# An RWKV time-mixing kernel on one Trainium2 core: small copies and memsets from VectorE to GpSimd, loads one unit sooner, one store placed after a transpose instead of ahead of it

## The chip, the cores and the metric

The kernel runs on one core of a Trainium2 chip. The metric is the device time of one execution in microseconds (us). Work is spread over TensorE (PE in the profile, with its weight loads as PEld), VectorE (DVE), ScalarE (ACT), GpSimd (POOL) and SyncE (SP); transfers are issued by SP, ACT and POOL and carried by the core's 16 DMA engines.

## The reference

```python
batch, seq_len, d_model = (16, 2048, 256)
x_prev[:, 1:, :] = x[:, :-1, :]          # x_prev[:, 0, :] = 0
xv = x * time_mix_v + x_prev * (1 - time_mix_v)
xr = x * time_mix_r + x_prev * (1 - time_mix_r)
v = xv.reshape(-1, d_model) @ value_weight
r = xr.reshape(-1, d_model) @ receptance_weight
out = (1 / (1 + np.exp(-r)) * v) @ output_weight
```

The key branch of the model does not reach the output. Input and output are fp32, 32 MB each way in all.

## The kernel before, in words

The 16 batches are cut into 64 units of 512 tokens, four units to a batch. A unit needs x transposed, with the 256 channels on partitions in two halves (`ko`), because the three projections contract over channels. It also needs each token's predecessor. The transposed tile `xt` therefore keeps a row of slots of 128 tokens, and one additional slot, slot 0 of the row, that holds the last slot shifted by one token. Its first column is the zero that stands before a sequence (a memset, L224 for batches 0 and 1, L221 later); its other 127 columns are copied from the last slot by `wrap_slots` (L528), the "shifted slot" of the title.

Three stages make `xt`. Batches 0 and 1 are loaded unit by unit (L171, L189, L149), batches 2 to 9 whole (L159), and TensorE transposes them into PSUM (L297 and L269), from where ScalarE copies them (L302, L279, L286). Batches 10 to 15 are loaded as bf16 into DRAM (`x_natural`, L155 and L159) and transposed by two DMA transposes (L251), one for batches 10 to 12, issued in the pass g = 27, one for 13 to 15, in g = 39.

In the pass g of the main loop TensorE computes the receptance product of unit g (L364, `psum_r`), ScalarE its sigmoid (L629), TensorE the value product (L364, `psum_v`) and the output product of the unit before (L393, `psum_o`), ScalarE copies the output (L442) and SP stores it, two units at a time (L445, L411). The mixing is folded: x times a coefficient plus x_prev. VectorE makes one half of the scaling (L334), GpSimd the other (L344), and VectorE adds (L356) and multiplies sigmoid and value (L668). For unit 0 the receptance product is made from x and x_prev directly (`project_unmixed`, L378), which reads slots 0 to 3 of `xt[0]`.

Every engine executes in the order in which the code lists its instructions: the order is written out by hand (`tc.manual_schedule()`), and semaphores make an instruction wait for what it reads. So it matters where a statement stands. `new_xt(0)`, which holds the memset of slot 0 of batch 0, is called after the early loads:

```python
    for e in (2, 3):
        op = nc.gpsimd.dma_start(out=x_first[:, e - 2], ...)     # L189
        if e == 2:
            tc.add_manual_dep(op.ins, first_weight.ins.name, SYNC, ...)
    nc.gpsimd.dma_start(out=wo_bf, ...)                           # L192
    load(1)                                                       # L149, four transfers
    ...
    warm_up(WARM)                                                 # TensorE
    ...
    new_xt(0)                                                     # L224
```

The dependency on `first_weight` makes the first of these GpSimd transfers wait until the receptance weight has landed. `first_transposes`, with the transposes of unit 0, and then L549 (the weight of x_prev), L334, L356 and L378 follow.

In the late part, `STAGE_AT` says in which pass g the loads of batches 13 to 15 are issued; each waits for the first DMA transpose. `FIRST` lists the stores (by the unit that completes them) that are issued on SP ahead of a transpose, and that wait for half of the last load; `WAITING` lists those that are held until the transpose has been issued.

Of the kernel before, what the change touches and what calls it, by code (L numbers as in the profile page):

```python
# [15 lines left out]
def kernel(  # L16
# [25 lines left out]
    nc = tc.nc  # L42
# [10 lines left out]
    BYUNIT = 2  # L53
# [5 lines left out]
    FREE = CROSS  # L59
    LATE_O = CROSS - 2  # L60
    T_AT = {27: 10, 39: 13}
    FIRST = {21: 27, 27: 39, 29: 39}
    WAITING = {23: 27, 25: 27, 31: 39, 33: 39, 35: 39}
    ZEROS_AT = 12
    STAGE_AT = {33: 13, 34: 14, 35: 15}
    GROUPS = [(2, 3), (4, 5, 6), (7, 8, 9), (10, 11, 12), (13, 14, 15)]
    HALVED = (12, 15)
    PAD = 16
# [3 lines left out]
    AHEAD = 6  # L72
# [38 lines left out]
    xt = {}  # L111
# [2 lines left out]


    zeros = consts.tile([P, P], BF16)
    nc.vector.memset(zeros, 0.0)
    ident_f = consts.tile([P, P], FP32)
    make_identity(nc, ident_f)
    ident = consts.tile([P, P], BF16)  # L120
    nc.vector.tensor_copy(out=ident, in_=ident_f)

    def rows(b):
        return x[b].rearrange("(p j) d -> p j d", p=P)
# [39 lines left out]
    for m, tm in enumerate([time_mix_r, time_mix_v]):  # L164
        nc.scalar.dma_start(
            out=tm_rows[m * KO : (m + 1) * KO, :], in_=tm.rearrange("(ko p) -> ko p", p=P)
        )

    def load_halves(e):
# [8 lines left out]
        out=w_f32[:, 0], in_=receptance_weight.rearrange("(ko p) n -> p ko n", p=P)  # L178
# [28 lines left out]
    def new_xt(b):  # L207
        if b >= BYUNIT:
            for group in GROUPS:
                if b != group[0]:  # L210
                    continue
                if b >= STAGED:
                    t = xtpool.tile([P, KO, len(group) * (PAD + S)], BF16, name="xt_both")
                    for k in range(len(group)):
                        xt[b + k] = t[:, :, k * (PAD + S) + PAD - 1 : (k + 1) * (PAD + S)]
                    xt_both[b] = t
                    return
                xt_both[b] = xtpool.tile([P, J + 1, KO, len(group), P], BF16, name="xt_both")
                for k in range(len(group)):
                    xt[b + k] = xt_both[b][:, :, :, k]  # L220
                    nc.gpsimd.memset(xt[b + k][:, 0, :, 0:1], 0.0)  # L221
            return
        xt[b] = consts.tile([P, UB * (UJ + 1), KO, P], BF16, name=f"xt_first{b}")
        (nc.vector if b == 0 else nc.gpsimd).memset(xt[b][:, 0, :, 0:1], 0.0)  # L224

    new_xt(0)
    tms = consts.tile([P, 2, KO], FP32)
# [83 lines left out]
    def slots(piece, off=0):  # L311

        b, _, lo, hi = piece
        j = lo // P + (lo // TU if b < BYUNIT else 0) + off
        return slice(j, j + (hi - lo) // P)
# [56 lines left out]
    def project_unmixed(ps, mo):  # L372


        parts = [(w_prev[:, ko], ko, 0) for ko in range(KO)]
        parts += [(w_bf[:, 0, ko], ko, 1) for ko in range(KO)]
        for n, (w, ko, lo) in enumerate(parts):
            nc.tensor.matmul(  # L378
                out=ps[:, mo, :],
                lhsT=w[:, mo * P : (mo + 1) * P],  # L380
                rhs=xt[0][:, lo : lo + UJ, ko],
                start=(n == 0),
                stop=(n == len(parts) - 1),
            )
# [45 lines left out]
    def output(g, z):  # L430
# [19 lines left out]
        elif e % 2 == 1:  # L450
            pair = (b, (e - 1) * UJ, (e + 1) * UJ)
            if g in FIRST:
                firsts.setdefault(FIRST[g], []).append(pair)
            elif g in WAITING:
                kept.setdefault(WAITING[g], []).append(pair)
            else:
# [47 lines left out]
    def pieces(g):  # L504

        b, e = divmod(g, UB)
        tile_for(g // 2)
        return [(b, m, e * TU, (e + 1) * TU) for m in range(2)]

    def wrap_slots(piece, one=None, after=None):  # L510


        b, _, lo, _ = piece
        by_unit = b < BYUNIT
        key = (b, lo // TU if by_unit else UB - 1)
        if key not in late_copies:
            return
        kos = slice(0, KO) if one is None else slice(one, one + 1)
        if one in (None, KO - 1):
            late_copies.remove(key)  # L520
        j = slots(piece).start if by_unit else 0
        n = UJ if by_unit else J
        if by_unit and j > 0:
            engine = nc.vector if key == (0, 1) else nc.gpsimd
            engine.tensor_copy(out=xt[b][:, j, kos, 0:1], in_=xt[b][:, j - 1, kos, P - 1 : P])
        if key in shifted:
            return
        op = (nc.vector if after is None else nc.gpsimd).tensor_copy(  # L528
            out=xt[b][:, j, kos, 1:P], in_=xt[b][:, j + n, kos, 0 : P - 1]
        )  # L530
        if after is not None:
            tc.add_manual_dep(op.ins, after.ins.name, SYNC, reason="one at a time")
# [4 lines left out]
    def advance(limit):  # L537
        nonlocal tnext
        while tnext <= min(limit, NU - 1):
            b, e = divmod(tnext, UB)  # L540
            for n in LOADS.get((b, e), ()):
                loads[n] = load(n)
            if tnext < NU - BYDMA:
                transposes(tnext)
            tnext += 1

    first_transposes()
    for ko in range(KO):
        nc.vector.tensor_scalar(  # L549
            out=w_prev[:, ko, :],  # L550
# [6 lines left out]
        out=w_bf[:, 0, 0, :], in0=w_f32[:, 0, 0, :], scalar1=tms[:, 0, 0:1], scalar2=None, op0=ALU.mult  # L557
    )
    nc.scalar.activation(
        out=w_bf[:, 0, 1, :], in_=w_f32[:, 0, 1, :], func=ACT.Copy, scale=tms[:, 0, 1:2]  # L560
# [3 lines left out]
    for ko in range(KO):  # L564
        nc.vector.tensor_scalar(
            out=w_bf[:, 1, ko, :],
# [13 lines left out]
    pooled = {g: [] for g in range(-1, NU)}  # L580
# [36 lines left out]
    for g in range(NU - 1):  # L617
        ps_r = ps_r_pool.tile([P, KO, TU], FP32, name="psum_r")
        if g == 0:
            project_unmixed(ps_r, 0)  # L620
            advance(1)
            project_unmixed(ps_r, 1)
            wrap_slots(pieces(1)[0])
            scale(pieces(1)[0])
            last = add(pieces(1)[0])
        else:
            project(ps_r, g, 0)
        s_sb = zpool.tile([P, KO, TU], BF16, name="s_sb")
        nc.scalar.activation(out=s_sb, in_=ps_r, func=ACT.Sigmoid)  # L629
        advance(START_T[g] if g < len(START_T) else g + LOOK)  # L630
        if g in T_AT:
            half, whole = loads[T_AT[g] + 2]
            for pair in firsts.pop(g):
                store(nc.sync, *pair, after=half)
            last_t = by_dma(T_AT[g], whole)
            for pair in kept.pop(g, []):
                store(nc.sync, *pair)
        if LATE_O < g < NU - 2:
            output(g - 2, z_prev2)
        for p in products.get(g + 1, []):  # L640
            if g >= FREE and p[0][1] == 1:
                scale_act(p[0], (0,))
        for p in [q for q, _ in products[g]] + pooled[g]:
            last_unit_of = p[3] // TU - 1
            need = last_unit_of if p[0] < BYUNIT else min(last_unit_of + 1, UB - 1)
            assert UB * p[0] + need < tnext, (g, p, tnext)
            if g > AHEAD or p not in pooled[g]:
                wrap_slots(p)
        if g == 1:
            load(2)  # L650
            scale_act(pieces(2)[1], (1,))
        for p, kos in products[g]:
            if not (g - 1 >= FREE and p[1] == 1):
                scale(p, kos)
        for p in sums[g]:
            last = add(p)
        for p in pooled[g]:
            if p[0] >= BYUNIT:
                wrap_slots(p)
        ps_v = ps_v_pool.tile([P, KO, TU], FP32, name="psum_v")  # L660
        project(ps_v, g, 1)
        if g == 0:
            scale_act(pieces(1)[1], (0,))
            advance(2)
        z_sb = zpool.tile([P, KO, TU], BF16, name="z_sb")
        n = TU // 2 if g == NU - 2 else TU
        for c in range(0, TU, n):
            nc.vector.tensor_tensor(  # L668
                out=z_sb[:, :, c : c + n],
                in0=s_sb[:, :, c : c + n],  # L670
                in1=ps_v[:, :, c : c + n],
                op=ALU.mult,
            )
        for p in pooled[g]:
            wrap_slots(p, after=last)
            scale_pool(p, last)
        if ZEROS_AT <= g < ZEROS_AT + len(pads):
            zero_rows(*pads[g - ZEROS_AT])
        if g in STAGE_AT:
            b = STAGE_AT[g]  # L680
            loads[b] = load(b)
            for op in loads[b] if b in HALVED else [loads[b]]:
                tc.add_manual_dep(op.ins, last_t.ins.name, SYNC, reason="not beside transposes")
        for p in held[g]:
            add(p)
        if z_prev is not None and not LATE_O <= g < NU - 3:
            output(g - 1, z_prev)
        if g == 1:
            advance(4)
        z_prev2, z_prev = z_prev, z_sb  # L690
# [31 lines left out]
```

## Time and profile before

| what | value |
|---|---|
| median of 3 runs | 200.48 us (200.44 to 200.55) |
| the profiled execution | 201.01 us, of which the span from the first to the last instruction is 199.2 us |
| PE, DVE, ACT, POOL busy | 192.5, 184.4, 177.0, 86.9 us |
| granted TensorE clock, mean | 0.995 |
| DMA | 58.13 MB, mean 292 GB/s |

The span is 1.8 us shorter than the time of the same execution; that part lies around the program and is taken as fixed. Busy times are unions over an engine's instructions, so a busy share near 100% says that the engine had always something under way, not that it ran at its peak.

### The profile page before, as it was taken

What the parts mean: (1) busy time and instruction counts of PE and PEld (TensorE: products, weight loads), DVE (VectorE), ACT (ScalarE), POOL (GpSimd) and SP (SyncE); (2) the same over time, 40 slices, a digit from 0 to 9 for tenths busy, and PEclk for the clock granted to TensorE, in tenths of its full rate; (3) what the DMA queues carried; (4) which work ended last, traced back from release to release, by engine and by line L of the source; (5) the groups of instructions that cost most, each with busy time, mean ns of one, the idle gap of its engine ahead of it and who ended that gap; (6) DMA issues with size and microseconds to landing.
All of it is one profiled execution on the core that took longest, in us unless ns stands there. A gap on an engine that the chain in (4) does not pass through costs nothing.

```text
span 199.2 us, 3758 instructions
## 1 busy us (share of the span) xinstructions
PE 192.5 (97%) x1368; PEld 123.5 (62%) x1368; DVE 184.4 (93%) x289; ACT 177.0 (89%) x197; POOL 86.9 (44%) x115
## 2 busy tenths in 40 slices
PE   8999999999999999999999999999999999999990
PEld 3555676666666666666666556666666666666660
DVE  0899999999999999999999999999999999999960
ACT  3699899999999999999999999999999999999970
POOL 1656452453675635524424366444444444444200
PEclk9999999999999999999999999999999999999998
DMA  5799999999999999999999999999999999999994
GB/s 177 203 187 215 215 280 275 278 282 274 286 312 332 285 285 331 296 268 211 296 250 290 367 276 207 209 280 295 198 238 346 416 421 400 409 399 407 409 392 177
DMA packets 37961, 58.13 MB, mean 292 GB/s; under 512 B 26068, under 2 KB 27448, under 8 KB 35128
## 3 DMA queue, kind: packets, MB, share of 16 engines
q1 hardware_dynamic: 33392, 41.34, 60.7%
q0 software_dynamic: 4400, 16.44, 41.6%
q8 instruction: 10, 0.16, 0.3%
q10 hardware_dynamic: 152, 0.13, 0.2%
q14 instruction: 7, 0.06, 0.1%
HBM read 34.34 MB, written 39.90 MB: 373 GB/s over the span
## 4 chain that ended last, share of the span: by engine, by line
PE 88%; ACT 4%; DMA 2%; issue 2%; DVE 1%; SPq 0%; DVEq 0%
PE psum_v L364 26%; PE psum_o L393 26%; PE psum_r L364 26%; PE ps_t L269 8%; DMA w_f<-n_receptance_weight_dram 2%; ACT xt_first L286 1%; ACT s_sb L629 1%; PE psum_r L378 1%; PE ps_t L393 1%; ACT mix L609 1%; ACT o_sb L442 1%; PE ps_t L364 0%; SPq L171 0%; DVE z_sb L668 0%; DVE mix L356 0%
## 5 line engine op out<-in xcount | busy, mean ns | idle before, releaser
L344 POOL TENSOR_SCALAR mix<-xt_both,c_sb 128x1024 bf16<-128x1024 bf16 (+1 forms) x55 | 61.3, 1114 | 84.7 <-DVE mix L356 82.8
L356 DVE TENSOR_TENSOR mix<-mix,xt_both 128x1024 bf16<-128x1024 bf16 x112 | 77.4, 701 | 1.4
L668 DVE TENSOR_TENSOR z_sb<-s_sb,psum_v 128x1024 bf16<-128x1024 bf16 (+1 forms) x64 | 76.7, 1200 | 1.9 <-PE psum_v L364 0.8
L364 PEld LDWEIGHTS <-w_bf 128*128 128x128 bf16 x516 | 49.0, 98 | 38.7 <-DVE mix L356 0.5
L629 ACT ACTIVATE s_sb<-psum_r 128x1024 bf16<-128x1024 f32 x63 | 65.2, 1035 | 6.2 <-PE psum_r L364 6.0
L364 PE MATMUL psum_v<-mix,w_bf 128*128 128x512 bf16 (+1 forms) x256 | 65.3, 377 | 0.1
L364 PE MATMUL psum_r<-mix,w_bf 128*128 128x512 bf16 (+1 forms) x252 | 64.2, 377 | 0.0
L393 PE MATMUL psum_o<-wo_bf,z_sb 128*128 128x256 bf16 x486 | 63.4, 273 | 0.2 <-DVE z_sb L668 0.2
L393 PEld LDWEIGHTS <-z_sb 128*128 128x128 bf16 x512 | 51.7, 103 | 18.2 <-DVE z_sb L481 0.7
L442 ACT COPY o_sb<-psum_o 128x1024 f32<-128x1024 f32 x50 | 51.2, 1024 | 5.0 <-PE psum_o L393 5.0
L286 ACT COPY xt_both<-ps_t 128x1024 bf16<-128x1024 bf16 x32 | 32.8, 1036 | 0.0
L269 PEld LDWEIGHTS <-x_bf 128*128 128x128 bf16 x304 | 19.7, 98 | 8.9 <-DMA x_bf<-in_x_dram 1.5
L269 PE MATMUL ps_t<-ident,x_bf 128*128 128x128 bf16 x304 | 22.7, 219 | 0.3 <-DMA x_bf<-in_x_dram 0.3
L334 DVE TENSOR_SCALAR mix<-xt_both,c_sb 128x1024 bf16<-128x1024 bf16 (+1 forms) x47 | 21.1, 458 | 0.0
L609 ACT ACTIVATE mix<-xt_both,c_sb 128x1024 bf16<-128x1024 bf16 x14 | 16.3, 1161 | 0.0
L356 DVE TENSOR_TENSOR mix<-mix,xt_first 128x1024 bf16<-128x1024 bf16 x15 | 10.6, 713 | 0.1
L442 ACT COPY x_bf<-psum_o 128x1024 f32<-128x1024 f32 x10 | 10.2, 1015 | 0.0
L334 DVE TENSOR_SCALAR mix<-xt_first,c_sb 128x512 bf16<-128x512 bf16 x22 | 6.5, 348 | 0.3 <-ACT xt_first L279 0.2
L286 ACT COPY xt_first<-ps_t 128x1024 bf16<-128x1024 bf16 x6 | 6.2, 1027 | 0.0
L159 POOL DMA_DIRECT2D x_bf<-in_x_dram x8 | 5.7, 712 | 0.0
L528 POOL COPY xt_first<-xt_first 128x254 bf16<-128x254 bf16 x5 | 2.0, 395 | 6.6 <-DVE mix L356 6.6
L344 POOL TENSOR_SCALAR mix<-xt_first,c_sb 128x512 bf16<-128x512 bf16 x6 | 4.1, 689 | 0.7 <-DVE mix L356 0.2
(70 smaller groups left out, 54.0 us busy)
## 6 DMA issues: line engine op xcount, KB each, us to landing
out_dram<-o_sb SPq DMA_DIRECT2D x24, 1024.0 KB, 14.1
x_bf<-in_x_dram POOLq DMA_DIRECT2D x8, 1024.0 KB, 20.6
x_natural<-in_x_dram POOLq DMA_DIRECT2D x4, 1024.0 KB, 13.3
out_dram<-x_bf SPq DMA_DIRECT2D x4, 1024.0 KB, 13.1
x_natural<-in_x_dram POOLq DMA_DIRECT2D x4, 512.0 KB, 15.2
x_bf<-in_x_dram POOLq DMA_DIRECT2D x6, 256.0 KB, 6.1
out_dram<-x_bf SPq DMA_DIRECT2D x6, 256.0 KB, 4.2
o_sb<-in_x_dram SPq DMA_DIRECT2D x4, 256.0 KB, 4.0
```

Of the source, the lines that this page charges most:

```text
L159: return nc.gpsimd.dma_start(out=x_bf[b], in_=rows(b), max_dma_last_dim=run)
L269: nc.tensor.transpose(out=ps[:, jj], in_=src[:, jj, ko * P : (ko + 1) * P], identity=idn)
L286: nc.scalar.copy(out=xt[b][:, j0 : j0 + UJ], in_=ps)
L334: nc.vector.tensor_scalar(out=mixed(piece)[:, :, ko], in0=tokens(piece, 0, ko), scalar1=c_sb[:, m, ko : ko + 1], scalar2=None, op0=ALU.mult,)
L344: op = nc.gpsimd.tensor_scalar(out=mixed(piece)[:, :, 1], in0=tokens(piece, 0, 1), scalar1=c_sb[:, m, 1:2], scalar2=1.0, op0=ALU.mult, op1 ...
L356: return nc.vector.tensor_tensor(out=mixed(piece), in0=mixed(piece), in1=tokens(piece, 1), op=ALU.add)
L364: nc.tensor.matmul(out=ps[:, mo, :], lhsT=w_bf[:, m, ko, mo * P : (mo + 1) * P], rhs=mixed((b, m, e * TU + lo, e * TU + hi))[:, :, ko], st ...
L393: nc.tensor.matmul(out=ps[:, j, :], lhsT=slot[:, ko, j], rhs=wo_bf[:, ko, :], start=(ko == 0), stop=(ko == KO - 1),)
L442: nc.scalar.copy(out=o[:, j0 : j0 + UJ, :], in_=ps)
L609: nc.scalar.activation(out=mixed(piece)[:, :, ko], in_=tokens(piece, 0, ko), func=ACT.Copy, scale=c_sb[:, m, ko : ko + 1],)
L629: nc.scalar.activation(out=s_sb, in_=ps_r, func=ACT.Sigmoid)
L668: nc.vector.tensor_tensor(out=z_sb[:, :, c : c + n], in0=s_sb[:, :, c : c + n], in1=ps_v[:, :, c : c + n], op=ALU.mult,)
```

## The change

Five edits. The zero tile's memset (L117), the cast of the identity to bf16 (L121) and the memset of slot 0 of batch 0 (L224) go from VectorE to GpSimd, at the same places in the code. The shifted slots of batches 3 to 9 are no longer copied by VectorE ahead of its scaling but by GpSimd, right ahead of GpSimd's own scaling and after the pass's last addition (`after=last`). `STAGE_AT` issues the loads of batches 13, 14 and 15 in passes 32, 33, 34 instead of 33, 34, 35. The store of the pair that ends with unit 29 goes from `FIRST` to `WAITING`: on SP it stands after the second transpose instead of ahead of it.

```diff
-    FIRST = {21: 27, 27: 39, 29: 39}
-    WAITING = {23: 27, 25: 27, 31: 39, 33: 39, 35: 39}
+    FIRST = {21: 27, 27: 39}
+    WAITING = {23: 27, 25: 27, 29: 39, 31: 39, 33: 39, 35: 39}
     ZEROS_AT = 12
-    STAGE_AT = {33: 13, 34: 14, 35: 15}
+    STAGE_AT = {32: 13, 33: 14, 34: 15}
...
     zeros = consts.tile([P, P], BF16)
-    nc.vector.memset(zeros, 0.0)
+    nc.gpsimd.memset(zeros, 0.0)
     ident_f = consts.tile([P, P], FP32)
     make_identity(nc, ident_f)
     ident = consts.tile([P, P], BF16)
-    nc.vector.tensor_copy(out=ident, in_=ident_f)
+    nc.gpsimd.tensor_copy(out=ident, in_=ident_f)
...
         xt[b] = consts.tile([P, UB * (UJ + 1), KO, P], BF16, name=f"xt_first{b}")
-        (nc.vector if b == 0 else nc.gpsimd).memset(xt[b][:, 0, :, 0:1], 0.0)
+        nc.gpsimd.memset(xt[b][:, 0, :, 0:1], 0.0)
...
-            if g > AHEAD or p not in pooled[g]:
+            if p not in pooled[g] or g > AHEAD and p[0] < BYUNIT:
                 wrap_slots(p)
...
         for p in sums[g]:
             last = add(p)
-        for p in pooled[g]:
-            if p[0] >= BYUNIT:
-                wrap_slots(p)
         ps_v = ps_v_pool.tile([P, KO, TU], FP32, name="psum_v")
...
         for p in pooled[g]:
             wrap_slots(p, after=last)
             scale_pool(p, last)
```

## The prediction

> **What bounds the kernel now.** I read the chain that ended last first, then busy times by stretch, then the start instruction by instruction, then the late DMA. The chain:
>
> ```profile
> PE 88%; ACT 4%; DMA 2%; issue 2%; DVE 1%; SPq 0%; DVEq 0%
> ...
> 30.00:50.00 20.00, 20.00 (x162) 13.31 (x161) 19.79 (x34) 19.80 (x22) 8.01 (x12) 1.00 1.05 277
> 150.00:160.00 10.00, 10.00 (x64) 6.44 (x62) 9.95 (x15) 9.19 (x11) 4.49 (x4) 1.00 1.09 388
> 197.00:198.00 1.00, 0.00 (x0) 0.00 (x0) 0.00 (x0) 0.00 (x0) 0.00 (x0) 0.63 0.08 27
> ```
>
> The columns of the last three are the stretch, its length, then PE, PEld, DVE, ACT and POOL busy, granted clock, DMA share, GB/s. From 30 us to 190 us PE is never idle, and one pass takes 3.05 us with transposes and 2.60 us without, pass after pass; DVE is 96 to 99% busy beside it. So PE bounds the middle: DVE work removed there shortens nothing, and anything that delays PE's start is not made up later. Now the start, PE, then DVE, then POOL (start, duration; in brackets the idle time before and its releaser):
>
> ```profile
> 5.76 0.73 PE L201 MATMUL ps_t<-const-bfloat16-1.0 128*128 128x512 bf16 x4
> 6.72 0.65 PE L378 MATMUL psum_r<-xt_first,w_prev 128*128 128x512 bf16 x2 [0.23 <-DVE w_prev L549]
> ...
> 1.53 0.06 DVE L224 MEMSET xt_first<- 128x2 bf16 x1
> 7.11 0.61 DVE L334 TENSOR_SCALAR mix<-xt_first,c_sb 128x512 bf16<-128x512 bf16 x2
> ...
> 6.59 1.29 POOL L189 DMA_DIRECT2D x_bf<-in_x_dram  x2 [5.27 <-DMA w_f<-n_receptance_weight_dram]
> 7.87 0.74 POOL L192 DMA_DIRECT2D wo_bf<-in_output_weight_dram  x1
> 8.58 2.17 POOL L149 DMA_DIRECT2D x_bf<-in_x_dram  x4
> 10.98 0.69 POOL L344 TENSOR_SCALAR mix<-xt_first,c_sb 128x512 bf16<-128x512 bf16 x1 [0.24 <-DVE mix L356]
> ```
>
> The memset of slot 0 is done at 1.6 us, on a DVE with nothing else to do, and PE begins its real work at 6.72. POOL sits until 6.59 waiting for the weight and then issues seven DMAs without a pause, until 8.58 + 2.17 = 10.75.
>
> The late DMA, on SP's queue:
>
> ```profile
> 99.00 11.61 SPq L251 DMA_TRANSPOSE xt_both<-x_natural  x1
> 110.70 21.45 SPq L411 DMA_DIRECT2D out_dram<-o_sb  x4
> 133.90 17.23 SPq L251 DMA_TRANSPOSE xt_both<-x_natural  x1
> 151.18 2.15 SPq L411 DMA_DIRECT2D out_dram<-o_sb  x3
> ```
>
> The second transpose has two 1 MB stores ahead of it, issued at 131.3 and 131.8, and takes 5.6 us longer than the first. From 160 us on stores land every 2.43 us per MB (162.4, 164.8, 167.2 ...) until 198.06: the DMA works off a backlog to the very end. DVE's last copy ends at 194.6, the last store is issued at 195.07, after SP's earlier ones, and lands 3.0 us later.
>
> **What the Trainium skill says.** "TensorE: Matmul & The Clock Gate", specifications: GpSimd's queue is strict FIFO, so a memset listed behind DMA issues runs behind them. The trace agrees: batch 1's memset (L224, 15.52) runs at its place between L344 and the next L159. Same page, "What's actually happening": after about one idle window of 3.4 us, whose boundaries run free, the array falls to half clock, and a busy window is needed to get back. Here the clock falls once, at 197.26, which is 3.1 us after PE's last matmul, and before 6.11 us the 512-column warm-up matmuls come 0.41 us apart, later ones 0.216: both agree. "SBUF — State Buffer", "Who interferes with whom": a VectorE operation with two SBUF inputs contends with a GpSimd one that reads SBUF. The trace has the shifted copy at 395 ns on POOL beside such work, at 218 on DVE. "DMA: Bandwidth & Descriptors", "Issuing engines are not separate DMA queues": loads, stores and transposes interleave on 16 engines, as the longer second transpose agrees.
>
> **The change part by part.**
>
> *Memset of slot 0 to POOL.* It removes 0.06 us from an idle DVE. On POOL it stands behind L189 x2, L192 and L149 x4, whose first waits for the weight. It starts at 10.75, takes 0.10 (the POOL memset of the same shape at 15.52), and is seen by another engine 0.1 later: 10.95. Two instructions read that column: the first matmul of L378 and the first L334. Behind L378 the whole of PE is queued (unit 0's projection, the transposes of unit 1); behind L334 all of DVE. Both stand from about 6.5 to 10.95. PE starts 10.95 - 6.72 = 4.2 us late; the short wait inside L378 for L556 and L559 is gone by then (0.1), so **4.1 us**. Later PE gaps of this start (0.14, 0.47, 0.23, 0.2 us between 10 and 23) stem mostly from DVE, which is 98% busy there and just as late: I recover nothing. POOL's and ACT's next steps wait for DVE and PE and move along. Bounds: 3.5 us if all gaps of DMA data (0.47) and half of the rest go, 4.3 if none.
>
> *The clock.* PE now idles from 6.5 to 10.95, 4.4 us, longer than the 3.1 us that it took at the end. From 6.11 in steps of 3.41 the boundaries of the profiled run are 9.52, 12.94, 16.35 (197.26 is the 56th). The stretch 6.11 to 9.52 would be 89% idle: half clock from 9.52. If the stretch to 12.94, about 60% busy, counts as busy, PE runs 2.0 us at half clock and loses 1.0; if not, 5.4 us and 2.7, of which about 0.4 falls into its own gaps. The boundaries need not stand there in another execution: with others the half clock lasts 2.4 to 3.4 us (1.2 to 1.7 lost), or doesn't come. I take 1.3; ends 0 and 2.3.
>
> *L117 and L121 to POOL.* A memset and a cast, by the nearest POOL rows (memset 0.20 for ident_f, select 0.29) about 0.15 and 0.3 us, end before 2.1 us. They are covered by POOL's wait until 6.59; ident_f, later by 0.15, is needed by L297 at 3.64, the zeros by ACT at 2.89. Cost 0. If POOL's wait were gone they would delay its seven issues by 0.45.
>
> *Seven shifted slots to POOL.* DVE loses 7 x 218 ns = 1.5 us, all between 39.8 and 112.4, where PE is never idle: gain 0 (at most 0.2). POOL gains 7 x (0.395 + 0.1 to the next) = 3.5 us, in idle stretches of 1.6 to 2.3 us ahead of each L344. Example: after the addition that ends at 89.54, POOL would copy from 89.71 to 90.10 and scale from 90.20 to 91.32; DVE's scaling at 91.29 reads the slot, its addition at 91.69 the product. 0.4 us to spare, cost 0. Without that, each of seven passes would delay DVE by up to 0.2: at most 1 us, less its own 1.5.
>
> *Loads one unit sooner, one store moved.* POOL issues load 13 after the L344 of one pass before (about 112.3 instead of 115.0 on the old clock); its wait for the first transpose (landed 112.70) could hold POOL 0.4 us, less than its idle time. The second transpose has one store less beside it: 17.23 - 2.4 = 14.8 us, and starts sooner. Batch 13 is first read by POOL at 155.45, so nothing waited and nothing is gained on PE. The moved store keeps its buffer longer, until about 153 plus the delay of the start; its buffer is next filled near 161 plus the delay: no wait (0 to 1 us). The sum of DMA work is unchanged.
>
> *The end.* The queue of loads never ran empty before (a load lands every 7 to 9 us with the next issued), so DMA does not lose what PE loses: relative to PE it gains most of the 4 to 5 us. The backlog should be gone before the last stores. Then SP issues the last one at 194.7 in 0.33 instead of from 195.07 in 0.68, and it lands some 2 us later, about 197.0 instead of 198.06: **-1.0** (ends -1.3 and 0).
>
> Sum: 4.1 + 1.3 + 0 - 1.0 = **+4.4** on the span of 199.2: 203.6, and 201.01 + 4.4 = 205.4 for that execution, which was 0.53 above the median of its kernel: 200.48 + 4.4 = **204.9 us**.
>
> **The rivals.**
>
> *The clock doesn't fall* (0.24): 4.1 - 1.0 = +3.1, 203.6 us. For it: boundaries run free, and without a mostly idle window in the 4.4 us there is no drop. Against: 3.1 us were enough at the end.
>
> *Half clock for two windows* (0.22): 4.1 + 2.3 - 1.0 = +5.4, 205.9; 206.9 if the tail returns nothing. For it: the profile's own boundaries, and that the first partly filled window at the start (0.78 to 2.70) did not raise the clock.
>
> *The start's wait is no wait* (0.05, not slower): the new semaphore wait of L378 and L334 could be met by earlier POOL work, or the seven issues could end by 6.6. Then only the DMA parts and DVE's 1.5 us count: -1.0 to 0, 199.5 to 200.5. It decides if L378 starts before 7 us. Against: the memset follows load(1) in the code, POOL is in order, and L378 reads its column.
>
> *Main forecast* (0.49): +3.8 to +5.0, 204.3 to 205.5.
>
> **How the numbers follow.** About 0.2% (0.4 us) is what a measurement of this kernel can tell from no change. All but the fourth case are slower by far more: slower 0.95, same 0.02, faster 0.03. The range takes in the first rival down to 203.2 (a gap more recovered) and the second up to 206.6.
>
> **What would show it.** Right: POOL's L224 at 10.7 to 10.9, L378 right after it with some 4.2 us idle before, released by POOL; a PEclk below 1 near 10 to 16 us; passes of 3.05 and 2.60 us afterwards; L528 on POOL x12 with DVE's L356 not waiting for it; last landing closer to the last issue. Wrong: L378 at 6.7, or PE gaps after 30 us, or a wait of ACT's L442 for a store near 165.

## The result and the profile after

The changed kernel takes 206.19 us (median of 6 runs, 205.29 to 206.79), the kernel before 200.59 us beside it (6 runs). The ratio is 1.0276, 95% interval 1.0251 to 1.0301: slower by 5.6 us, where 4.4 was forecast (204.9 us, range 203.2 to 206.6). The profiled execution took 206.12 us, with a span of 204.2 us against 199.2 us before.

The start, from the timelines of PE, DVE and POOL of the changed kernel (start, duration, instruction, in brackets the idle time before and its releaser):

```profile
5.38 0.56 PE L201 MATMUL ps_t<-const-bfloat16-1.0 128*128 128x512 bf16 x4
10.35 1.01 PE L378 MATMUL psum_r<-xt_first,w_prev 128*128 128x512 bf16 x2 [4.42 <-POOL xt_first L224]
...
10.33 0.62 DVE L334 TENSOR_SCALAR mix<-xt_first,c_sb 128x512 bf16<-128x512 bf16 x2 [3.69 <-POOL xt_first L224]
...
5.97 1.34 POOL L189 DMA_DIRECT2D x_bf<-in_x_dram  x2 [4.18 <-DMA w_f<-n_receptance_weight_dram]
7.30 0.74 POOL L192 DMA_DIRECT2D wo_bf<-in_output_weight_dram  x1
8.01 2.17 POOL L149 DMA_DIRECT2D x_bf<-in_x_dram  x4
10.11 0.18 POOL L224 MEMSET xt_first<- 128x2 bf16 x1
```

A memset of 0.18 us releases both TensorE and VectorE, after 4.42 and 3.69 us in which neither did anything. It could not run earlier: seven DMA issues stand ahead of it on GpSimd, and the first of them waited for a weight that landed at 5.67.

Busy time by stretch, from the changed kernel (stretch, length, busy PE, PEld, DVE, ACT, POOL, granted clock, DMA share, GB/s):

```profile
8.20:10.30 2.10, 0.00 (x0) 0.00 (x0) 0.00 (x0) 0.00 (x0) 2.10 (x5) 0.51 1.10 191
10.30:15.10 4.80, 4.75 (x16) 2.85 (x16) 2.67 (x9) 1.17 (x2) 0.00 (x0) 0.50 1.11 172
...
30.00:50.00 20.00, 20.00 (x172) 13.68 (x171) 19.83 (x35) 19.56 (x23) 9.39 (x18) 1.00 1.05 278
```

The clock falls to half at 8.26 us, while TensorE waits, and comes back at 15.09, so nearly all the work of the first 4.7 us after the wait runs at half speed. From 30 to 190 us TensorE is idle for 0.14 us in all (before: never), so nothing of the start is made up.

SP's late queue in the changed kernel:

```profile
135.78 0.33 SPq L411 DMA_DIRECT2D out_dram<-o_sb  x1
138.35 11.93 SPq L251 DMA_TRANSPOSE xt_both<-x_natural  x1
...
199.24 1.92 SPq L411 DMA_DIRECT2D out_dram<-x_bf  x4
```

One store instead of two ahead of the second transpose, and 11.93 us for its issue instead of 17.23. The last store lands at 203.02, 2.2 us behind VectorE's last copy (end 200.79); before it was 3.45 us behind.

How the 5.0 us of span come about: L378 starts 3.63 us later (10.35 for 6.72); from there to the first value product it takes 4.91 us for 2.71, another 2.20; later passes lose 0.35 more (VectorE's last copy ends 6.18 us later in all); and the end returns 1.2.

In all that follows a ratio compares undisturbed runs alone while a median takes in every run, so the two can differ.

### The profile page after: what moved, and what is told of

It reads as the page before. It is cut to its first block, busy times and chain, and to the rows that moved or that the text cites. A ratio compares the mean times of both kernels' runs of the same rounds, so it can differ in the third digit from the quotient of the medians.

```text
span 204.2 us, 3764 instructions
## 1 busy us (share of the span) xinstructions
PE 194.4 (95%) x1368; PEld 124.6 (61%) x1368; DVE 185.5 (91%) x279; ACT 176.7 (87%) x197; POOL 90.2 (44%) x125
## 4 chain that ended last, share of the span: by engine, by line
PE 41%; DVE 35%; ACT 10%; issue 7%; POOL 3%; DMA 2%; SPq 0%; DVEq 0%
DVE z_sb L665 15%; DVE mix L356 14%; PE psum_v L364 13%; PE psum_o L393 12%; PE psum_r L364 12%; DVE mix L334 5%; ACT s_sb L629 4%; ACT xt_both L286 3%; ACT o_sb L442 3%; DMA w_f<-n_receptance_weight_dram 2%; PE psum_r L378 2%; PE ps_t L269 1%; POOL x_bf L149 1%; PE ps_t L393 1%; POOL x_bf L189 1%
## 5 line engine op out<-in xcount | busy, mean ns | idle before, releaser
L356 DVE TENSOR_TENSOR mix<-mix,xt_both 128x1024 bf16<-128x1024 bf16 x112 | 80.3, 727 | 1.4
L609 ACT ACTIVATE mix<-xt_both,c_sb 128x1024 bf16<-128x1024 bf16 x14 | 16.3, 1161 | 0.0
L528 POOL COPY xt_both<-xt_both 128x254 bf16<-128x254 bf16 x7 | 2.8, 393 | 11.8 <-DVE mix L356 11.8
L279 ACT CAST xt_first<-ps_t 128x512 bf16<-128x512 f32 x2 | 1.2, 585 | 6.9 <-PE ps_t L269 6.9
L378 PE MATMUL psum_r<-xt_first,w_prev 128*128 128x512 bf16 x4 | 2.1, 622 | 4.4 <-POOL xt_first L224 4.4
```

The source lines that it names most:

```text
L356: return nc.vector.tensor_tensor(out=mixed(piece), in0=mixed(piece), in1=tokens(piece, 1), op=ALU.add)
L378: nc.tensor.matmul(out=ps[:, mo, :], lhsT=w[:, mo * P : (mo + 1) * P], rhs=xt[0][:, lo : lo + UJ, ko], start=(n == 0), stop=(n == len(part ...
L609: nc.scalar.activation(out=mixed(piece)[:, :, ko], in_=tokens(piece, 0, ko), func=ACT.Copy, scale=c_sb[:, m, ko : ko + 1],)
```

## The experiments

Each ratio is to runs of the kernel before on the same chip; its median there was 200.40 us for the first four experiments, 200.87 for the next three, 201.06 for the next three, 200.87 for the last two. Single executions of one kernel spread by up to 4.2 us in these series, and each label has one profiled execution.

**The memset alone** (`e1_memset_alone`), on the kernel before:

```diff
-        (nc.vector if b == 0 else nc.gpsimd).memset(xt[b][:, 0, :, 0:1], 0.0)
+        nc.gpsimd.memset(xt[b][:, 0, :, 0:1], 0.0)
```

> The kernel before with one edit: the memset of slot 0 of batch 0 on GpSimd, at its place behind the seven DMA issues. Theory (late start plus half clock): the whole loss is here, 205.0 to 207.0 us, L378 waiting 3.6 to 4.4 us for POOL's L224, and some 3 to 7 us of half clock. Rival (the start is made up later, the shifted copies on GpSimd or the DMA order cost the time): 200.3 to 201.5 us.

205.79 us, ratio 1.0293 (1.0249 to 1.0337): the loss of the whole change, from one line. Its waits:

```profile
PE psum_r L378 <- POOL xt_first L224: 4.4, 1, 4.4
DVE mix L334 <- POOL xt_first L224: 3.7, 1, 3.7
```

(Who waited for whom, total us, times, longest.) Half clock lasted from 9.07 to 15.90.

**The memset back on VectorE, all else changed** (`e2_memset_back`):

```diff
-        nc.gpsimd.memset(xt[b][:, 0, :, 0:1], 0.0)
+        (nc.vector if b == 0 else nc.gpsimd).memset(xt[b][:, 0, :, 0:1], 0.0)
```

> The changed kernel with this memset back on VectorE, all other edits kept. Theory: the loss is gone, L378 starts near 6.2 to 6.8 us, 199.5 to 200.8 us; of the other edits only the DMA order could move the end, by 0 to -1.0. Rival (shifted copies or DMA order cost the time): 204 us or more.

200.78 us, ratio 1.0014 (0.9991 to 1.0036), L378 at 6.25. The loss is gone; no gain is left over either.

**The memset on GpSimd, but ahead of its DMA issues** (`e3_memset_ahead`), on the changed kernel:

```diff
+    xt[0] = consts.tile([P, UB * (UJ + 1), KO, P], BF16, name="xt_first0")
+    nc.gpsimd.memset(xt[0][:, 0, :, 0:1], 0.0)
     for e in (2, 3):
         op = nc.gpsimd.dma_start(out=x_first[:, e - 2], in_=unit_rows(x, 0, e)[:, 0])
...
-    new_xt(0)
```

> The changed kernel, the memset still on GpSimd but listed ahead of its first early load (L189) instead of behind the last. If the place in the queue is what costs: as with the memset on VectorE, 199.5 to 200.8 us, POOL's memset near 1.8 us. If the engine is what costs (a slow GpSimd memset, or a late signal from GpSimd): 203 us or more.

200.44 us, ratio 1.0007 (0.9985 to 1.0028). GpSimd's timeline (the added lines move L189 to L191):

```profile
1.74 0.10 POOL L189 MEMSET xt_first<- 128x2 bf16 x1
6.50 1.29 POOL L191 DMA_DIRECT2D x_bf<-in_x_dram  x2 [4.66 <-DMA w_f<-n_receptance_weight_dram]
```

The same instruction on the same engine costs nothing at 1.74 us. It is the place in the queue that cost 5 us, not GpSimd.

**TensorE kept busy while it waits** (`e4_keep_warm`), on the changed kernel:

```diff
-    WARM2 = 7
+    WARM2 = 67
```

> The changed kernel with WARM2 = 67 instead of 7: some 3.3 us of additional warm-up matmuls in the time in which TensorE waits for the memset, so that the clock isn't lowered. They add no wait as long as they end before about 10.3 us. Theory (the half clock is a part of its own, 1.3 to 2.3 us): 203.0 to 204.9 us, clock 1.0 from 6 us on, L378 still near 10.4 to 11.0. Rival (the clock doesn't matter since VectorE sets the pace of these passes): 205.5 to 207 us, as the changed kernel.

204.19 us, ratio 1.0203 (1.0172 to 1.0235). PE's timeline:

```profile
5.50 3.84 PE L201 MATMUL ps_t<-const-bfloat16-1.0 128*128 128x512 bf16 x19
10.62 0.59 PE L378 MATMUL psum_r<-xt_first,w_prev 128*128 128x512 bf16 x2 [1.28 <-POOL xt_first L224]
```

And its busy time by stretch (columns as in the result above; the clock is the third figure from the end):

```profile
10.50:15.00 4.50, 4.38 (x30) 2.72 (x30) 3.89 (x11) 2.66 (x5) 0.30 (x2) 1.00 1.13 192
```

L378 starts no sooner, but the clock stays full from 4.84 us on, and the loss is 3.8 us instead of 5.4 to 5.6: the half clock is a part of its own, of 1.6 to 1.8 us in the medians. Only the wait and the end's gain are left.

**Half the queue** (`e7_half_queue`): on the changed kernel, the memset as in the third experiment, but between L192 and `load(1)`, behind three DMA issues.

> The changed kernel with the memset listed between L192 and the four transfers of L149, so behind three of the seven DMA issues: it should run 2.1 us sooner, near 8.0 to 8.6, and TensorE wait some 1.5 to 2.3 us. If the loss is the wait plus a clock that falls only after a mostly idle stretch of 3.4 us: 201.7 to 203.0 us, clock full throughout in the profile. If each microsecond of wait costs alike (5.6 us for 4.2): 202.8 to 203.6.

203.28 us, ratio 1.0080 (1.0050 to 1.0111); the medians differ by 2.4 us. It doesn't tell the readings apart: the median fits a loss that goes with the wait, while the ratio, which stands for 1.6 us, fits the other reading. And in the profile TensorE ran at half speed until 12.12, as pairs of matmuls of one shape show (L379 is L378 here, moved by the added lines):

```profile
9.75 1.06 PE L379 MATMUL psum_r<-xt_first,w_bf 128*128 128x512 bf16 x2
12.66 0.59 PE L379 MATMUL psum_r<-xt_first,w_bf 128*128 128x512 bf16 x2
```

In this execution x landed late (1.0 us of wait in the transposes), the warm-up had a hole, and the clock had not risen at all before the wait. My expectation of a full clock was wrong for it. The memset ran at 8.75, 1.4 to 1.7 us ahead of where it ran in the first experiment and in the changed kernel.

**The shifted slots alone** (`e5_slots_alone`), on the kernel before:

```diff
-            if g > AHEAD or p not in pooled[g]:
+            if p not in pooled[g] or g > AHEAD and p[0] < BYUNIT:
                 wrap_slots(p)
...
-        for p in pooled[g]:
-            if p[0] >= BYUNIT:
-                wrap_slots(p)
```

> The kernel before with one edit: the seven shifted slots of batches 3 to 9 on GpSimd. The prediction's step: 1.5 us taken off VectorE, nothing on the path, 200.2 to 200.6 us. A second reading, from the trace of the changed kernel: GpSimd's scaling now ends 0.5 us later and VectorE's next addition is held until then (L356 mean 727 ns instead of 701), so that VectorE gains nothing and TensorE loses 0.2 to 0.5 us near the end of the transposing passes: 200.5 to 201.1 us, L356 near 725 ns.

201.03 us, ratio 1.0007 (0.9974 to 1.0040): no difference in time. VectorE's largest group of additions, in the kernel before and then here (busy us, mean ns, idle before):

```profile
L356 DVE TENSOR_TENSOR mix<-mix,xt_both 128x1024 bf16<-128x1024 bf16 x112 | 77.4, 701 | 1.4
...
L356 DVE TENSOR_TENSOR mix<-mix,xt_both 128x1024 bf16<-128x1024 bf16 x112 | 80.4, 729 | 1.4
```

The 1.5 us of copies leave VectorE and 3.0 us come back as longer additions.

**The DMA edits alone** (`e6_dma_alone`: the three changed lines of `FIRST`, `WAITING`, `STAGE_AT`), **the sooner loads alone** (`e8_loads_alone`: `STAGE_AT`), **the moved store alone** (`e9_store_alone`: `FIRST` and `WAITING`), and **the DMA edits with the zero tile and the identity on GpSimd** (`e10_dma_and_consts`: also L117 and L121), all on the kernel before.

> The kernel before with the DMA edits alone: loads 13 to 15 one pass sooner, one store behind the second transpose. If these edits make the end's gain: last landing some 2.2 to 2.6 us after VectorE's last copy instead of 3.45, 199.4 to 200.2 us. If the gain of the end came from the late start (DMA running ahead), as the prediction had it: 200.2 to 200.7 us, the last landing again some 3.4 us behind.

> The kernel before with only the loads of batches 13 to 15 one pass sooner; both stores stay ahead of the second transpose. If the sooner loads let the end catch up: second transpose 0 to 2.4 us sooner, last landing less than 2.6 us behind VectorE's last copy. If it is the moved store: as before, about 3.4 us behind, ratio 0.999 to 1.002.

> The kernel before with only the store of unit 29's pair behind the second transpose. The transpose should take 12 to 15 us instead of 17.2. If the moved store is what lets the end catch up: last landing less than 2.6 us behind VectorE's last copy, ratio 0.994 to 0.999. If it is the sooner loads: about 3.4 us behind, ratio 0.999 to 1.002.

> The DMA edits together with the zero tile's memset and the identity's cast on GpSimd, memset of slot 0 and shifted slots on VectorE. The prediction has the two moves at nothing: the same as the DMA edits alone, ratio 0.994 to 0.999. A rival, that they delay GpSimd's first DMA issues: 0.45 us more.

| kernel | median us | ratio, 95% interval | last landing behind VectorE's last copy, us |
|---|---|---|---|
| before (first profile) | 200.48 | | 3.45 |
| DMA edits | 199.95 | 0.9968 (0.9943 to 0.9992) | 2.03 |
| loads alone | 201.28 | 0.9972 (0.9944 to 1.0000) | 2.67 |
| store alone | 200.01 | 0.9951 (0.9928 to 0.9973) | 2.54 |
| DMA edits and constants | 200.10 | 0.9952 (0.9930 to 0.9974) | 2.03 |
| memset alone | 205.79 | 1.0293 (1.0249 to 1.0337) | 3.13 |

In these profiles each DMA edit alone lets the end catch up by about 0.8 to 0.9 us, both together by 1.4. For both together VectorE's last copy ends where it did before (194.54 us for 194.61), so it is the last store that lands sooner. For the loads alone a gain in time isn't shown: the interval reaches 1.0000, and the median lies above the 201.06 us of the kernel before beside it. With only the moved store the transpose, here on SP's timeline, is as short as in the changed kernel:

```profile
135.71 11.59 SPq L251 DMA_TRANSPOSE xt_both<-x_natural  x1
```

The constants on GpSimd cost nothing: the rival's 0.45 us does not appear.

**Slots on GpSimd beside slots on VectorE, same chip.** The DMA edits and the constants once more (`e11_slots_vector`), and the same plus the slots, which is the second experiment's kernel (`e12_slots_gpsimd`). The question was why that kernel shows no gain when the DMA edits alone do.

> The kernel with the DMA edits and the constants on GpSimd once more, on one chip beside the next, which differs from it by the seven shifted slots alone. Ratio to the kernel before 0.993 to 0.998.

> The changed kernel with the memset of slot 0 back on VectorE once more. If the slots on GpSimd are free, as the prediction had it: within 0.2% of the kernel beside it. If they cost (VectorE's longer additions and TensorE's short waits for them): 0.2 to 0.6% above it, 0.3 to 1.1 us; in the trace more waits of L364 for L356, 0.9 us instead of 0.4.

200.12 us, ratio 0.9949 (0.9926 to 0.9973), against 201.04 us, ratio 1.0004 (0.9976 to 1.0031): with the sooner loads, the slots on GpSimd cost 0.9 us. The reason is not the one expected; GpSimd, DVE and PE in `e12_slots_gpsimd`:

```profile
110.28 1.12 POOL L344 TENSOR_SCALAR mix<-xt_both,c_sb 128x1024 bf16<-128x1024 bf16 x1 [1.63 <-DVE mix L356]
114.61 0.57 POOL L159 DMA_DIRECT2D x_natural<-in_x_dram  x1 [3.21 <-DVE z_sb L665]
115.18 0.41 POOL L528 COPY xt_both<-xt_both 128x254 bf16<-128x254 bf16 x1
115.69 1.93 POOL L344 TENSOR_SCALAR mix<-xt_both,c_sb 128x1024 bf16<-128x1024 bf16 x1
...
115.62 0.48 DVE L334 TENSOR_SCALAR mix<-xt_both,c_sb 128x1024 bf16<-128x1024 bf16 x1 [0.46 <-POOL xt_both L528]
...
119.45 0.69 DVE L356 TENSOR_TENSOR mix<-mix,xt_both 128x1024 bf16<-128x1024 bf16 x1 [1.01 <-POOL mix L344]
...
121.33 1.02 PE L364 MATMUL psum_v<-mix,w_bf 128*128 128x512 bf16 x4 [0.68 <-DVE z_sb L665]
```

Load 13 (L159 at 114.61), one pass sooner, must wait for the first DMA transpose, which in this execution landed at 114.07 (the releaser in brackets is one that had long been done). GpSimd stands for 3.21 us, and batch 9's shifted slot and scaling, queued behind, are late; VectorE waits for both, TensorE for VectorE. From 110 to 130 us TensorE is busy 18.84 us of 20. In `e11_slots_vector` the transpose landed at 112.31, load 13 went out at 112.84, and TensorE was busy all 20 us. In `e8_loads_alone`, with the slots on VectorE, a landing at 113.69 held load 13 until 114.22, and TensorE was busy 19.40 us. The kernel of `e12_slots_gpsimd` was also profiled as `e2_memset_back`, in an execution of 199.91 us for 201.14. There the transpose landed at 111.57, and GpSimd stood for a quarter of the time:

```profile
112.11 0.57 POOL L159 DMA_DIRECT2D x_natural<-in_x_dram  x1 [0.78 <-DMA xt_both<-x_natural]
```

TensorE was busy 19.85 us of the same 20. So both edits bear on one pass, and in these profiles the cost goes with the landing of the transpose. That this is also what spreads the runs of these kernels, and all of the 0.9 us, is likely and not shown, since two executions of each kernel were profiled and no more.

The fastest versions are the kernel before with the moved store alone or with both DMA edits, with the constants moved or not: 0.3 to 0.5% less than the kernel before, with intervals that leave out 1.

## Why the prediction was right, and where it was not

*The memset behind the DMA issues* held in each step. From the first issue to L378 I had 10.95 - 6.59 = 4.36 us; it took 10.35 - 5.97 = 4.38. That the profiled stall came 0.6 us sooner is the weight, landed at 5.67 instead of 6.29: L378 starts 3.63 us late by the clock of the profiles, about 4.25 by that of the weight, for the 4.1 to 4.2 of the sum. "I recover nothing" held too: in `e4_keep_warm`, without half clock, L378 is 3.90 us late, VectorE's last copy 4.13.

*The clock* was the mis-sized term: 1.3 us taken, with 2.3 as its end; the trace shows 2.2, the medians 1.6 to 1.8. The main forecast, 204.3 to 205.5 us, was therefore missed, and the range held because it took in the second rival, half clock for two windows, priced at 205.9 us with 0.22: that is what came. The Trainium skill, "TensorE: Matmul & The Clock Gate", "What's actually happening", speaks of a window of 3.4 us. The half clock here lasted 6.83 us, twice 3.41, with boundaries at 4.85, 8.26, 11.67 and 15.09; the window to 8.26 was 32% busy and let the clock fall, the one to 11.67 39% busy and didn't bring it back. In `e1_memset_alone` 54% wasn't enough either. I should have given this rival more weight, since in the profile before a window that was 56% busy, the one up to 2.70, had not raised the clock.

*L117 and L121* cost nothing, as said. *The shifted slots*: nothing on the path of their own, as said, but not for the reason given. "DVE loses 1.5 us" failed. In the pass at 119 us GpSimd scales from 120.14 to 121.25, and the addition that follows VectorE's multiplication takes long. The corresponding scaling and addition before the change, then the pass at 119 us:

```profile
89.71 1.12 POOL L344 TENSOR_SCALAR mix<-xt_both,c_sb 128x1024 bf16<-128x1024 bf16 x1 [2.03 <-DVE mix L356]
...
90.60 0.77 DVE L356 TENSOR_TENSOR mix<-mix,xt_both 128x1024 bf16<-128x1024 bf16 x1
...
119.65 0.39 POOL L528 COPY xt_both<-xt_both 128x254 bf16<-128x254 bf16 x1 [1.53 <-DVE mix L356]
120.14 1.11 POOL L344 TENSOR_SCALAR mix<-xt_both,c_sb 128x1024 bf16<-128x1024 bf16 x1
...
120.70 1.10 DVE L356 TENSOR_TENSOR mix<-mix,xt_both 128x1024 bf16<-128x1024 bf16 x1
```

The late addition ends at 121.80, 0.55 us after GpSimd's scaling; the one before the change, begun at 90.60, ended at 91.37, 0.54 us after a scaling that ended at 90.83. No addition of this group that overlaps a scaling, in either kernel, ends sooner than 0.53 us after it, and one that meets neither a scaling nor a copy takes 0.68 to 0.69 us. In the changed kernel seven additions take 1.10 to 1.24 us, as many as there are shifted slots, and before the change one did. That fits the Trainium skill, "SBUF — State Buffer", "Who interferes with whom": the later of two such operations stands until the first is done. I had cited that section and priced only the copy, not the addition that GpSimd's later scaling would hold up. Nor did the 395 ns beside 218 show such a hold: all twelve of these copies take 0.39 us on GpSimd in the changed kernel.

*Loads and store*: that PE gains nothing from them held. What they do at the end was missed: *the end*, 1.0 us forecast, 1.2 measured in the profile, came by another cause than I gave, so the agreement is luck. I had the DMA running ahead because TensorE is late. With the late start alone the loads and the transpose move along (second transpose at 139.68, still 17.72 us long) and the last landing stays 3.13 us behind; the DMA edits alone bring it to 2.03. A small lateness can do it as well: in `e5_slots_alone` TensorE lost 1.76 us to late data at its start, the transpose began at 133.85 as ever, and the end stood at 2.04. And the hold of GpSimd by load 13, which I put at up to 0.4 us, was 0.8 to 3.2 in the profiles that have the sooner loads without the late start; in the changed kernel itself the late start hid it.

## What to carry to other kernels

Before an instruction is moved to another engine, list what stands ahead of it in that queue and what the first of those waits for: an engine with nothing to do may still have a blocked queue, and here that cost 5 us. A wait of 4.4 us on TensorE cost more than itself, because the work after it ran at half clock, for two windows, as the first was only 39 or 54% filled. An engine's busy time is no account from which a moved instruction is simply subtracted; look at which operations of the two engines can't run side by side, and at waits that two edits put into the same pass.

## What the runs showed of the hardware that I had not expected

With windows counted in steps of 3.41 us from the recorded changes of the clock, one that was 39% (changed kernel), 54% (`e1_memset_alone`) or 56% busy (before, at its start) did not raise the clock; it fell after one that was 32% busy and stayed up after one of 63% (`e4_keep_warm`). The busy share of the profile alone doesn't decide it: in `e7_half_queue` a window that was 85% busy, with its hole at the end (1.88 to 5.29), did not raise the clock, while 77% in `e10_dma_and_consts` and 83% in `e9_store_alone`, with the hole at the start, did. Why stays open. The landing of the same 256 KB weight, issued at 1.66 us in every execution, varied from 5.20 to 6.46 us, and GpSimd's first seven DMA issues with it. With two stores of 1 MB issued right ahead of the second DMA transpose its issue took 16.3 to 17.7 us, with one 11.6 to 14.4.
